# A causal mask added by VectorE in the maximum pass of an attention kernel, and a narrower last diagonal tile

## The chip, the cores and the metric

The kernel runs on one core of a Trainium2 chip. The metric is the device time of one execution in microseconds (us). Three runs of the kernel before gave 2625.49, 2625.82 and 2627.09 us; the median is 2625.82.

The engines are named as the profile names them: PE is TensorE (PEld its weight loads), DVE is VectorE, ACT is ScalarE, POOL is GpSimd, and SP is the queue that issues nearly all DMAs. Each engine works through its own queue in order and waits on semaphores for the others.

## The reference, cut to what matters

One decoder layer on 2048 tokens of 1024 channels: attention and a state-space model side by side, an output projection, a gated feed-forward network. Only the attention is touched here. It has 8 heads of 64 channels, is causal, and adds a forgetting bias to the scores:

```
cum = jnp.cumsum(log_f, axis=1).transpose(0, 2, 1)
...
    s = jnp.einsum('bqhd,bkhd->bhqk', q_i, k,
                   preferred_element_type=jnp.float32) * scale
    s = s + cum_i[..., :, None] - cum[:, :, None, :]
    mask = kpos[None, :] <= qpos[:, None]
    s = jnp.where(mask, s, NEG_INF)
    p = jax.nn.softmax(s, axis=-1)
    return jnp.einsum('bhqk,bkhd->bqhd', p.astype(v.dtype), v)
```

All data are float32, and the result has to be accurate to float32. So the kernel splits an operand into a high part of type float32r and the remainder, also as float32r, and multiplies the parts (high by high, high by low, low by high).

## The kernel before, in words

**Tiling.** The 2048 tokens are four blocks of 512 (`TB`). Attention is worked off by pairs of query block b and head h: 4 x 8 = 32 pairs, called heads below. For a pair the key blocks 0 to b are needed, the diagonal one (key block b) first.

**Two passes.** The softmax needs the row maximum before the exponentials.

- The *maximum pass*, `att_max` (L932 to L975), has scores with queries on the partitions. For each key block `ch` and each of four query tiles `s` of 128 rows, one matmul (L954) gives up to 512 key columns in a PSUM tile, from the high parts alone, with two more contraction rows that bring the forgetting bias. On the diagonal block only the first max(256, (s+1) x 128) columns are computed, and a second matmul (L958) adds the mask: it multiplies a bf16 identity, `identb`, by the bf16 tile `mask_q`, which holds 0 or -1e30, and accumulates into the columns s x 128 and on (256 columns wide for s = 0, otherwise 128). VectorE then takes the maximum of each row (L959) into a column of `mx`. `finish_max` (L961) reduces `mx` to the negated maximum, transposes it and stores it by DMA in row 66 of `qa`, so that the main pass subtracts it inside a matmul.
- The *main pass*, `att_main` (L979 to L1070), has scores with keys on the partitions. For each key block and each of four key tiles `i`, two matmuls (L997, L998) build scores minus maximum; on the diagonal block a third adds the mask from `mask_t`. There the columns start at `c0 = min(i * P, 256)`: 512, 384, 256 and 256 columns for i = 0 to 3. Tile i = 3 has only 128 valid columns; its mask (L1001) is 256 wide, and the first half of it is -1e30 throughout; the others use a mask of 128 columns (L1003). Then ScalarE takes the exponential into `pf` (L1007, two buffers) and makes its high part `ph` (L1008), VectorE makes the low part `pl` (L1009) and adds `pf` to the running row sums `acc` (L1014 for the first tile, L1017), and TensorE multiplies `ph` and `pl` by the values into `o_ps` (L1018, L1022).

**Score buffers.** Both passes take PSUM tiles from `am_ps` (L269): two buffers `sc_ps`, and from block 1 on also `qs_ps` and `vq_ps` in turn.

**What sets the order.** `attention` (L1072) writes out the order by hand: while a head is in its main pass, the steps of the next head's maximum pass are dealt out between its steps. Block 0's attention is emitted after the state-space model, which is issued at high priority, and stands beside it and the projections of blocks 2 and 3. The attention of blocks 1 to 3 (L1738) stands beside the output projection of block 0 and the first feed-forward matmuls (`up`, L1258), which fill TensorE between its steps. The whole program goes through a planner (`schedule_with_timeline_sim=True`, L1922): it puts the instructions of each engine in order by priority and by its own estimates of their times.

**Other lines named below.** L329: conditioning; L87: low part of a weight; L439 and L472: input projection, with L478 for the low part of queries and keys; L853, L859: state-space model; L555, L590: forget gates; L1147: GpSimd fills the constant rows of the tiles `qa`, `ka`, `kx`; L1048: reciprocals of the row sums; L1232, L1290 to L1292: output and down projections. `rsqrt_mean` (L172) is a chain of small VectorE operations.

Of the kernel before, what the change touches and what calls it, by code (L numbers as in the profile page):

```python
# [22 lines left out]
P = 128  # L23
# [11 lines left out]
NEG = -1e30  # L35
# [85 lines left out]
def hybrid_layer(ctx, tc, x, c_t, w_ada, b_col, gains, w_flat, bf_row, a_re, a_im, log_dt,  # L121
# [21 lines left out]
    identb = const.tile([P, P], BF16, name="identb")  # L143
# [5 lines left out]
    for g in range(2):  # L149
        G.memset(sel[g * 64 : (g + 1) * 64, g : g + 1], 1.0)  # L150

    mask_t = const.tile([P, 2 * P], BF16, name="mask_t")
    G.memset(mask_t, 0.0)
    G.affine_select(out=mask_t[:, P : 2 * P], in_=mask_t[:, P : 2 * P], pattern=[[1, P]],
                    compare_op=ALU.is_ge, fill=NEG, base=0, channel_multiplier=-1)
    G.memset(mask_t[:, 0:P], NEG)
    mask_q = const.tile([P, 2 * P], BF16, name="mask_q")
    G.memset(mask_q, 0.0)
    G.affine_select(out=mask_q[:, 0:P], in_=mask_q[:, 0:P], pattern=[[-1, P]],
                    compare_op=ALU.is_ge, fill=NEG, base=0, channel_multiplier=1)  # L160
    G.memset(mask_q[:, P : 2 * P], NEG)

    gain = const.tile([P, 32], F32, name="gain")
    Q.dma_start(gain, gains)
# [767 lines left out]
    def att_max(b, h):  # L932
# [16 lines left out]
        def part(ch, s):  # L949
            if s == 0:  # L950
                load(ch)
            n = max(256, (s + 1) * P) if ch == b else 512
            ps = max_ps()
            T.matmul(ps[:, 0:n], lhsT=qa[0:66, s * P : (s + 1) * P], rhs=ka[ch][0:66, 0:n], start=True,  # L954
                     stop=(ch != b))
            if ch == b:
                m0, mn = s * P, (2 * P if s == 0 else P)
                T.matmul(ps[:, m0 : m0 + mn], lhsT=identb, rhs=mask_q[:, 0:mn], start=False, stop=True)  # L958
            V.reduce_max(out=mx[:, s, ch : ch + 1], in_=ps[:, 0:n], axis=AX.X)  # L959

        def finish_max():  # L961
            mneg = small.tile([P, 4], F32, name="mneg", tag="mneg")
# [16 lines left out]
    def att_main(b, h, qa, qb, ka):  # L979
# [4 lines left out]
        def part(ch, i):  # L984
# [12 lines left out]
            T.matmul(ps[:, cs], lhsT=kbt[:, ks], rhs=qb[:, cs], start=True, stop=False)  # L997
            T.matmul(ps[:, cs], lhsT=ka[ch][:, ks], rhs=qa[:, cs], start=False, stop=(ch != b))  # L998
            if ch == b:
                if i == 3:  # L1000
                    T.matmul(ps[:, 256:512], lhsT=identb, rhs=mask_t, start=False, stop=True)  # L1001
                else:
                    T.matmul(ps[:, c0 : c0 + P], lhsT=identb, rhs=mask_t[:, P : 2 * P], start=False, stop=True)  # L1003
# [3 lines left out]
            A.activation(pf[:, cs], ps[:, cs], AF.Exp)  # L1007
            A.copy(ph[:, cs], pf[:, cs])  # L1008
            V.tensor_tensor(out=pl[:, cs], in0=pf[:, cs], in1=ph[:, cs].bitcast(F32), op=ALU.subtract)  # L1009
            first = state["first"]  # L1010
# [916 lines left out]
```

## Time and profile before

| what | value |
|---|---|
| median of 3 runs | 2625.82 us |
| profiled execution, its span | 2625.8 us |
| instructions | 35861 |
| mean granted TensorE clock | 0.980 |
| matmuls | 12235 |
| mask matmuls of the maximum pass (L958) | 128 |
| mask matmuls of the main pass (L1001, L1003) | 32 and 96 |
| maximum reductions (L959) | 320 |
| exponentials (L1007) | 320 |

The profiled execution took as long as the runs, so its durations can be set against the median as they are.

How the views are read. The page's first part gives for each engine the busy time, its share of the span and the instructions; the 40 slices show the busy share in tenths along the span. A row by line or by form gives the line, the engine, the operation, output <- inputs with their shapes, the count, the busy time and the mean of one in ns, and then the idle time just before these instructions with what ended it. A row of the waits gives who waited for whom, the total in us, how often and the longest. A row of one source line gives the minimum, median and maximum of one in ns and the first and last start. A row of the timeline begins with the start and the duration in us; for a matmul the duration runs from its start until its result is out, so that matmuls overlap in it, and what one costs the next is the distance between their starts.

### The profile page before, as it was taken

The page shows a single profiled execution, that of the slowest core. Times are in us where ns is not written, and L with a number is a line of the kernel's source. Part 1 is how long each engine was busy: PE and PEld are TensorE (multiplying, and loading weights), DVE is VectorE, ACT ScalarE, POOL GpSimd, SP SyncE. Part 2 cuts the span into 40 slices and gives each one's busy share as a digit, 9 for nine tenths or more (in the row PEclk, how much of TensorE's full clock was granted, in tenths as well). Part 3 has the DMA queues.
Part 4 walks back from the last instruction along what each step waited for, and adds up shares of the span by engine and source line. Part 5 has one row for each costly group of instructions (what it writes and reads, how often), then busy time and mean ns, then how long its engine had stood idle before and what let it go on. Part 6 is the DMA issues. An engine that isn't in the chain of part 4 may idle for free.

```text
span 2625.8 us, 35861 instructions
## 1 busy us (share of the span) xinstructions
PE 2539.7 (97%) x12235; PEld 2056.0 (78%) x12235; DVE 2043.4 (78%) x3824; ACT 1257.6 (48%) x2120; POOL 145.9 (6%) x130
## 2 busy tenths in 40 slices
PE   6999999998999999999999999999989999999997
PEld 3888877887788787888778888888767888887776
DVE  7989688966887878787877777776589888876777
ACT  3423255644454545455545555556554555543213
POOL 0001000000000000000000000000002333320000
PEclk8899999998999999999999999999999999999998
DMA  9476986667556655556557555556733443447573
GB/s 318 150 250 217 299 263 199 198 190 236 173 190 215 199 184 184 191 178 207 176 196 224 184 171 192 170 182 225 245 103 128 168 153 136 153 144 289 190 277 119
DMA packets 269319, 516.37 MB, mean 197 GB/s; under 512 B 27952, under 2 KB 114864, under 8 KB 269136
## 3 DMA queue, kind: packets, MB, share of 16 engines
q1 hardware_dynamic: 267312, 508.84, 58.4%
q0 software_dynamic: 1280, 4.20, 0.4%
q8 instruction: 97, 1.59, 0.3%
q10 hardware_dynamic: 544, 1.05, 0.1%
q14 instruction: 86, 0.70, 0.1%
HBM read 374.32 MB, written 139.59 MB: 196 GB/s over the span
## 4 chain that ended last, share of the span: by engine, by line
PE 80%; DMA 7%; DVE 7%; issue 2%; ACT 2%; SPq 1%; POOL 0%; DVEq 0%; POOLq 0%; ACTq 0%
PE ff_ps L1258 19%; PE up_x L1382 7%; PE ff_ps L1232 7%; PE up_z L1382 5%; PE up_y L1382 4%; PE ff_ps L1290 3%; PE ff_ps L1292 3%; PE ff_ps L1291 3%; PE o_ps L1018 2%; PE o_ps L1022 2%; DMA wada<-in_w_ada 2%; PE proj_ps L439 2%; PE acc_x L1612 2%; PE vq_ps L472 2%; PE qs_ps L472 2%
## 5 line engine op out<-in xcount | busy, mean ns | idle before, releaser
L86 ACT CAST w_hi<-w_raw 128x1024 fp32r<-128x1024 f32 (+4 forms) x187 | 173.1, 927 | 270.5 <-DMA w_raw<-in_w_flat 71.6
L1258 PE MATMUL ff_ps<-h_lo,w_hi 128*128 128x512 f32 x704 | 279.8, 397 | 0.8 <-DVE h_lo L391 0.8
L1258 PE MATMUL ff_ps<-h_hi,w_lo 128*128 128x512 f32 x704 | 280.0, 398 | 0.0
L1258 PE MATMUL ff_ps<-h_hi,w_hi 128*128 128x512 f32 x704 | 279.8, 399 | 0.0
L87 DVE TENSOR_TENSOR w_lo<-w_raw,w_hi 128x1024 fp32r<-128x1024 f32 (+4 forms) x187 | 199.8, 1069 | 64.4 <-ACT w_hi L86 52.5
L1009 DVE TENSOR_TENSOR pl<-pf,ph 128x512 fp32r<-128x512 f32 (+1 forms) x320 | 194.9, 618 | 19.8 <-ACT ph L1008 17.1
L1008 ACT CAST ph<-pf 128x512 fp32r<-128x512 f32 (+1 forms) x320 | 177.9, 569 | 62.4 <-PE o_ps L1018 56.4
L1017 DVE TENSOR_TENSOR acc<-acc,pf 128x512 f32<-128x512 f32 (+2 forms) x264 | 159.2, 605 | 26.0 <-ACT pf L1007 23.5
L1007 ACT ACTIVATE pf<-sc_ps 128x512 f32<-128x512 f32 (+2 forms) x184 | 98.3, 539 | 123.3 <-PE sc_ps L998 74.7
L1258 PEld LDWEIGHTS ff_ps<-h_lo,w_hi 128*128 128x128 f32 x704 | 133.6, 190 | 29.5 <-DVE h_lo L391 1.1
L1258 PEld LDWEIGHTS ff_ps<-h_hi,w_lo 128*128 128x128 f32 x704 | 133.5, 190 | 28.8
L1258 PEld LDWEIGHTS ff_ps<-h_hi,w_hi 128*128 128x128 f32 x704 | 133.4, 190 | 28.6 <-issue 0.2
L116 ACT CAST w_hi<-w_raw 128x1024 fp32r<-128x1024 f32 (+2 forms) x100 | 96.4, 964 | 103.7 <-PE ff_ps L1232 41.9
L1291 PE MATMUL ff_ps<-act_lo,w_hi 128*128 128x512 f32 x352 | 139.6, 397 | 0.0
L1290 PE MATMUL ff_ps<-act_hi,w_hi 128*128 128x512 f32 x352 | 139.4, 398 | 0.2 <-ACT rt L378 0.2
L1292 PE MATMUL ff_ps<-act_hi,w_lo 128*128 128x512 f32 x352 | 139.4, 397 | 0.0
L959 DVE TENSOR_REDUCE mx<-sc_ps 128x1 f32<-128x512 f32 (+2 forms) x164 | 97.6, 599 | 52.4 <-PE sc_ps L958 25.9
L1018 PE MATMUL o_ps<-ph,vv 128*128 128x512 f32 (+1 forms) x320 | 121.2, 380 | 2.2 <-ACT ph L1008 2.2
L1022 PE MATMUL o_ps<-pl,vv 128*128 128x512 f32 (+2 forms) x312 | 116.2, 375 | 0.9 <-DVE pl L1009 0.9
L1382 PE MATMUL up_x<-hh,w_hi 128*128 128x512 f32 x352 | 112.7, 400 | 3.4 <-ACT hh L387 1.8
L1364 POOL TENSOR_TENSOR s<-v_raw 128x512 f32<-128x512 f32 x18 | 27.7, 1538 | 1518.9 <-DVE w_lo L87 1518.9
L86 ACT CAST w_hi<-s 128x1024 fp32r<-128x1024 f32 (+2 forms) x66 | 62.1, 944 | 81.8 <-DVE s L1583 31.7
(678 smaller groups left out, 6961.1 us busy)
## 6 DMA issues: line engine op xcount, KB each, us to landing
w_raw<-in_w_flat SPq DMA_DIRECT2D x193, 512.0 KB
w_lo<-wlo SPq DMA_DIRECT2D x68, 512.0 KB
wlo<-w_lo SPq DMA_DIRECT2D x52, 512.0 KB
kb<-kb SPq DMA_DIRECT2D x80, 256.0 KB
vv<-v SPq DMA_DIRECT2D x80, 256.0 KB
w_raw<-in_w_flat SPq DMA_DIRECT2D x40, 384.0 KB
w_raw<-in_w_flat SPq DMA_DIRECT2D x40, 320.0 KB
wada<-in_w_ada SPq DMA_DIRECT2D x48, 256.0 KB
```

Source lines behind the costliest of these rows:

```text
L86: nc.scalar.copy(hi[:, :n], raw[:, :n])
L87: nc.vector.tensor_tensor(out=lo[:, :n], in0=raw[:, :n], in1=hi[:, :n].bitcast(F32), op=ALU.subtract)
L1008: A.copy(ph[:, cs], pf[:, cs])
L1009: V.tensor_tensor(out=pl[:, cs], in0=pf[:, cs], in1=ph[:, cs].bitcast(F32), op=ALU.subtract)
L1018: T.matmul(o_ps[:, cs], lhsT=vt[:, i, :], rhs=ph[:, cs], start=first, stop=False)
L1022: T.matmul(o_ps[:, cs], lhsT=vt[:, i, :], rhs=pl[:, cs], start=False, stop=(b > 0 and ch == b - 1 and i == 3))
L1232: mark[0] = T.matmul(ps, lhsT=lt, rhs=rt, start=(i == 0), stop=(i == 23))
L1258: T.matmul(ps, lhsT=lt, rhs=rt, start=(n == 0), stop=(n == 23))
L1290: T.matmul(ps, lhsT=a, rhs=ah[:, ts], start=(c == 0), stop=False)
L1291: T.matmul(ps, lhsT=a, rhs=al[:, ts], start=False, stop=False)
L1292: mark[0] = T.matmul(ps, lhsT=bb, rhs=ah[:, ts], start=False, stop=(c == n - 1))
L1382: mark[0] = T.matmul(ps, lhsT=lt, rhs=rt, start=(first and n == 0), stop=(n == 11), skip_group_check=not first)
```

## The change

In the maximum pass the mask matmul (L958) is gone. For the diagonal block VectorE adds `mask_q` to the scores in PSUM, writes the sum back in place and takes the maximum, in one instruction (`tensor_tensor_reduce`) on (s+1) x 128 columns. `mask_q` is now 512 columns wide, with the triangle in its last 128; its slice `(3 - s) * P` and on lines up with the query tile.

In the main pass the mask matmul of tile i = 3 is 128 wide, like the others. The exponential reads only the 128 valid columns of that tile, and GpSimd fills the other 128 of `pf` with zeros. `mask_t` is 128 columns wide. In `rsqrt_mean` two tiles have two buffers each, where they had four.

```
-    mask_t = const.tile([P, 2 * P], BF16, name="mask_t")
+    mask_t = const.tile([P, P], BF16, name="mask_t")
...
-    mask_q = const.tile([P, 2 * P], BF16, name="mask_q")
+    mask_q = const.tile([P, 4 * P], BF16, name="mask_q")
     G.memset(mask_q, 0.0)
-    G.affine_select(out=mask_q[:, 0:P], in_=mask_q[:, 0:P], pattern=[[-1, P]],
+    G.affine_select(out=mask_q[:, 3 * P :], in_=mask_q[:, 3 * P :], pattern=[[-1, P]],
                     compare_op=ALU.is_ge, fill=NEG, base=0, channel_multiplier=1)
-    G.memset(mask_q[:, P : 2 * P], NEG)
...
-        i = small.tile([P, 8], I32, name="rs_i")[:, :n]
+        i = small.tile([P, 8], I32, name="rs_i", bufs=2)[:, :n]
...
-            t = small.tile([P, 8], F32, name="rs_t")[:, :n]
+            t = small.tile([P, 8], F32, name="rs_t", bufs=2)[:, :n]
...
-            T.matmul(ps[:, 0:n], lhsT=qa[0:66, s * P : (s + 1) * P], rhs=ka[ch][0:66, 0:n], start=True,
-                     stop=(ch != b))
+            T.matmul(ps[:, 0:n], lhsT=qa[0:66, s * P : (s + 1) * P], rhs=ka[ch][0:66, 0:n], start=True, stop=True)
+            to = mx[:, s, ch : ch + 1]
             if ch == b:
-                m0, mn = s * P, (2 * P if s == 0 else P)
-                T.matmul(ps[:, m0 : m0 + mn], lhsT=identb, rhs=mask_q[:, 0:mn], start=False, stop=True)
-            V.reduce_max(out=mx[:, s, ch : ch + 1], in_=ps[:, 0:n], axis=AX.X)
+                sc = ps[:, 0 : (s + 1) * P]
+                V.tensor_tensor_reduce(out=sc, in0=sc, in1=mask_q[:, (3 - s) * P :], scale=1.0, scalar=3.0 * NEG,
+                                       op0=ALU.add, op1=ALU.max, accum_out=to)
+            else:
+                V.reduce_max(out=to, in_=ps[:, 0:n], axis=AX.X)
...
             if ch == b:
-                if i == 3:
-                    T.matmul(ps[:, 256:512], lhsT=identb, rhs=mask_t, start=False, stop=True)
-                else:
-                    T.matmul(ps[:, c0 : c0 + P], lhsT=identb, rhs=mask_t[:, P : 2 * P], start=False, stop=True)
+                T.matmul(ps[:, i * P : (i + 1) * P], lhsT=identb, rhs=mask_t, start=False, stop=True)
...
-            A.activation(pf[:, cs], ps[:, cs], AF.Exp)
+            e0 = i * P if ch == b else 0
+            if e0 > c0:
+                G.memset(pf[:, c0:e0], 0.0)
+            A.activation(pf[:, e0:], ps[:, e0:], AF.Exp)
```

More of the change, by code (lines that the diff above doesn't have):

```diff
@@ L150, in hybrid_layer @@
         G.memset(sel[g * 64 : (g + 1) * 64, g : g + 1], 1.0)
-    mask_t = const.tile([P, 2 * P], BF16, name="mask_t")
+    mask_t = const.tile([P, P], BF16, name="mask_t")
     G.memset(mask_t, 0.0)
-    G.affine_select(out=mask_t[:, P : 2 * P], in_=mask_t[:, P : 2 * P], pattern=[[1, P]],
-                    compare_op=ALU.is_ge, fill=NEG, base=0, channel_multiplier=-1)
-    G.memset(mask_t[:, 0:P], NEG)
-    mask_q = const.tile([P, 2 * P], BF16, name="mask_q")
+    G.affine_select(out=mask_t, in_=mask_t, pattern=[[1, P]], compare_op=ALU.is_ge, fill=NEG, base=0,
+                    channel_multiplier=-1)
+    mask_q = const.tile([P, 4 * P], BF16, name="mask_q")
     G.memset(mask_q, 0.0)
-    G.affine_select(out=mask_q[:, 0:P], in_=mask_q[:, 0:P], pattern=[[-1, P]],
+    G.affine_select(out=mask_q[:, 3 * P :], in_=mask_q[:, 3 * P :], pattern=[[-1, P]],
                     compare_op=ALU.is_ge, fill=NEG, base=0, channel_multiplier=1)
-    G.memset(mask_q[:, P : 2 * P], NEG)
     gain = const.tile([P, 32], F32, name="gain")
```

## The prediction

> **What bounds the kernel now.** I read the page from the top: busy time by engine, the 40 slices, the chain that ended last.
>
> ```profile
> PE 2539.7 (97%) x12235; PEld 2056.0 (78%) x12235; DVE 2043.4 (78%) x3824; ACT 1257.6 (48%) x2120; POOL 145.9 (6%) x130
> PE   6999999998999999999999999999989999999997
> PE 80%; DMA 7%; DVE 7%; issue 2%; ACT 2%; SPq 1%; POOL 0%; DVEq 0%; POOLq 0%; ACTq 0%
> ```
>
> TensorE is busy nearly everywhere and is four fifths of the chain. The edit touches attention alone, so the next view is the windows, cut at the attention of block 0 (313 to 650 us) and of blocks 1 to 3 (650 to 1830 us).
>
> ```profile
> core 0: us, PE busy (x) PEld busy (x) DVE busy (x) ACT busy (x) POOL busy (x), PEclk, DMA share, GB/s
> 0.00:313.00 313.00, 279.44 (x1669) 233.67 (x1670) 262.91 (x731) 101.73 (x202) 20.13 (x47) 0.93 0.75 244
> 313.00:650.00 337.00, 322.35 (x1866) 267.39 (x1865) 258.26 (x514) 166.26 (x338) 2.07 (x4) 0.96 0.74 224
> 650.00:1830.00 1180.00, 1172.79 (x5370) 941.48 (x5369) 903.95 (x1653) 645.61 (x1077) 0.00 (x0) 1.00 0.57 189
> 1830.00:2626.00 796.00, 765.08 (x3335) 613.49 (x3333) 618.31 (x926) 343.97 (x504) 123.75 (x79) 0.99 0.50 177
> ```
>
> From 650 to 1830 us TensorE rests 1180 - 1173 = 7 us, less than 1%, at a full clock; VectorE is busy 904 of 1180 (77%), ScalarE 646 (55%), GpSimd never. In block 0's attention TensorE has 322 of 337 (96%). The busy time of pipelined matmuls is modelled, so I also look at the waits of TensorE, first from 650 to 1830 us, then from 313 to 650 us (the longest lines).
>
> ```profile
> PE o_ps L1018 <- ACT ph L1008: 2.2, 2, 1.7
> PE o_ps L1022 <- DVE pl L1009: 0.9, 1, 0.9
> PE sc_ps L954 <- DVE mx L959: 0.8, 1, 0.8
> ```
> ```profile
> PE vq_ps L439 <- DVE qk_lo L478: 3.8, 2, 3.2
> PE qs_ps L954 <- DVE mx L959: 3.4, 1, 3.4
> ```
>
> TensorE waits for the maximum in two places, 4.2 us in all. So a matmul slot taken out of attention shortens the kernel, unless VectorE's or GpSimd's new work makes a new wait.
>
> **Part 1, the mask matmuls of the maximum pass.** L958 goes: one for each head and query tile, 32 x 4 = 128. This is its line of the code, by output buffer:
>
> ```profile
> L958 PE MATMUL sc_ps<-mask_q,identb x81: 219/232/287, 315.7 to 1717.3; 128*128 128x128 bf16 x61, 128*128 128x256 bf16 x20
> L958 PE MATMUL vq_ps<-mask_q,identb x25: 229/232/331, 629.3 to 1708.7; 128*128 128x128 bf16 x17, 128*128 128x256 bf16 x8
> L958 PE MATMUL qs_ps<-mask_q,identb x22: 230/231/285, 623.5 to 1656.6; 128*128 128x128 bf16 x18, 128*128 128x256 bf16 x4
> ```
>
> 81 + 25 + 22 = 128. Their 0.23 us is the time from start to result; matmuls overlap. What one costs TensorE is read from the distance between starts, in the timeline of TensorE at 1001 us:
>
> ```profile
> 1000.62 0.34 PE L998 MATMUL qs_ps<-qa,ka 67*128 67x384 f32 x1
> 1000.80 0.23 PE L1003 MATMUL qs_ps<-mask_t,identb 128*128 128x128 bf16 x1
> 1000.84 0.47 PE L1258 MATMUL ff_ps<-h_hi,w_hi 128*128 128x512 f32 x1
> 1001.16 0.28 PE L954 MATMUL sc_ps<-ka,qa 66*128 66x256 f32 x1
> 1001.28 0.28 PE L958 MATMUL sc_ps<-mask_q,identb 128*128 128x256 bf16 x1
> 1001.32 0.36 PE L954 MATMUL sc_ps<-ka,qa 66*128 66x256 f32 x1
> 1001.51 0.39 PE L1018 MATMUL o_ps<-ph,vv 128*128 128x512 f32 x1
> 1001.75 0.23 PE L958 MATMUL sc_ps<-mask_q,identb 128*128 128x128 bf16 x1
> 1001.78 0.48 PE L1258 MATMUL ff_ps<-h_lo,w_hi 128*128 128x512 f32 x1
> 1002.10 0.39 PE L1258 MATMUL ff_ps<-h_hi,w_lo 128*128 128x512 f32 x1
> 1002.33 0.40 PE L1258 MATMUL ff_ps<-h_hi,w_hi 128*128 128x512 f32 x1
> ```
>
> An undisturbed matmul of 512 columns holds its place 0.23 us (1002.10 to 1002.33), one of 256 columns 0.12 (1001.16 to 1001.28). A mask matmul is followed after 0.03 to 0.04 us, but the matmul behind it then holds its place longer: 1001.78 to 1002.10 is 0.32 instead of 0.23, and the one of 256 columns, 1001.32 to 1001.51, 0.19 instead of 0.12. Mask and follower together cost 1002.10 - 1001.75 - 0.23 = 0.12 us more, 1001.51 - 1001.28 - 0.12 = 0.11, and 1001.16 - 1000.80 - 0.23 = 0.13. I take 0.12 us, whatever the mask's width: the weights of the mask and of its follower have to go in behind a matmul too short to cover them. After a score matmul of only 256 columns without a mask (1001.16) no such loss shows, so nothing takes its place.
>
> The Trainium skill has another price for this: "TensorE: Matmul & The Clock Gate", section "Back-to-back issue gap", gives about 81 ns for a matmul of 128 columns with its weight load, by which the sum below would be 128 x 0.081 = 10.4 us (an estimate from that page). The distances between starts here are 0.11 to 0.13 us, so the trace decides against it.
>
> The sum: 32 of the 128 lie in block 0's attention, where TensorE sets the pace for 96% of the time: 32 x 0.12 x 0.96 = 3.7 us. The other 96 lie where it does for 99%: 96 x 0.12 x 0.99 = 11.4 us. Together 15.1 us off the path.
>
> **Part 2, the maximum on VectorE.** The mask is now added while the maximum is taken, on 128, 256, 384 and 512 columns instead of 256, 256, 384 and 512, and the sum is written back into PSUM. No row shows this instruction. Its neighbours:
>
> ```profile
> L959 DVE TENSOR_REDUCE mx<-sc_ps 128x1 f32<-128x512 f32 x103 | 70.5, 686 | 39.0 <-PE sc_ps L954 25.9 <-PE sc_ps L958 12.8
> L959 DVE TENSOR_REDUCE mx<-sc_ps 128x1 f32<-128x256 f32 x45 | 18.4, 417 | 4.6 <-PE sc_ps L958 4.4
> L853 DVE TENSOR_TENSOR m<-ss_ps,tab 128x512 f32<-128x512 f32 x16 | 11.0, 687 | 9.4 <-PE ss_ps L848 9.2
> L590 DVE TENSOR_TENSOR fg<-fg 128x128 fp32r<-128x128 f32 x1 | 0.3, 284 | 0.0
> L1048 DVE RECIPROCAL rd<-sc_ps 128x8 f32<-128x8 f32 x12 | 2.4, 203 | 1.3 <-PE sc_ps L1046 1.2
> ```
>
> A two-input operation with a PSUM input takes as long as the reduction (687 against 686 ns), so the pass over the columns costs the same, and the first tile saves 417 - 284 = 0.13 us: 32 x 0.13 = 4.3 us less VectorE time as the lower bound. The upper bound is a separate small step to write the maximum out, at the 0.20 us of L1048: 128 x 0.20 - 4.3 = 21 us more. I take the middle of these, about +9 us, since nothing is nearer to either end. Even +21 us raises VectorE in attention from (258 + 904) / 1517 = 77% to 78%, so the cover that hides it is TensorE's own work. What is queued behind it on VectorE are the `pl` and `acc` of the main pass, whose readers are TensorE and ScalarE; and the score buffer is released later by the same 0.1 us. TensorE's wait for that is 4.2 us now; scaled by 0.1 of 0.69 us it grows by 0.6, and the maximum starts earlier because no mask matmul comes between. I charge 0.3 us.
>
> On that extra step the Trainium skill speaks against the change: "VectorE: DVE Perf Modes", section "Two Vector instructions with no wait between them", says that an operation that also writes out its accumulator is two instructions. No row of this trace shows one; it argues for the upper half of the bounds, which the time does not feel as long as TensorE leads.
>
> **Part 3, the last diagonal key tile.** The mask there shrinks from 256 to 128 columns (32 matmuls, one a head). As seen above, a mask of 256 columns costs TensorE no more than one of 128, so nothing. The exponential reads 128 columns, not 256, and GpSimd fills the other 128 with zeros.
>
> ```profile
> L1007 ACT ACTIVATE pf<-sc_ps 128x512 f32<-128x512 f32 x123 | 73.2, 598 | 92.9 <-PE sc_ps L998 74.7 <-PE sc_ps L1003 7.5 <-DVE pl L1009 7.0
> L1007 ACT ACTIVATE pf<-sc_ps 128x256 f32<-128x256 f32 x41 | 15.7, 384 | 19.6 <-PE sc_ps L1001 12.2 <-DVE pl L1009 3.4 <-DVE acc L1014 2.1
> L555 POOL MEMSET fg<- 128x128 f32 x1 | 0.2, 199 | 13.2 <-DVE ada_acc L321 13.2
> ```
>
> The slope is (598 - 384) / 256 = 0.84 ns a column, so 128 columns take about 384 - 107 = 277 ns: 32 x 0.11 = 3.4 us less on ScalarE, which is not the bound: nothing. The fill takes 0.20 us, beside an exponential of 0.28, and both wait for the same release of `pf`: nothing, as long as GpSimd, idle here, has nothing ahead in its queue. If that cover is gone, it costs what rival 3 says. The masks themselves are built in the first microseconds; `rs_i` and `rs_t`, cut to two buffers, are a chain on one engine: nothing.
>
> **Sum.** The profiled execution lasted 2625.8 us, as does the median of the runs, so no correction between them. 2625.8 - 15.1 + 0.3 = 2611.0 us.
>
> **Rivals.** 1. *VectorE gives half back.* At the upper bound of 0.20 us a maximum, the score buffers come free later in the bursts where one head's four diagonal tiles follow each other. If 0.06 us of each 0.20 reaches TensorE: 128 x 0.06 = 7.7 us, so 2618 to 2619 us. For it: TensorE has waited for `mx` before. Against: only twice.
> 2. *Another order.* The kernel's order is planned anew from estimated times. TensorE rests 34 + 15 + 7 + 31 = 86 us over the four windows; an order that moves a tenth of that changes the time by 8 us either way: 2603 or 2619. If it loses all 15 us it ends at 2625: the change does nothing. That the slots were not TensorE's limit, its busy time being modelled, would give the same.
> 3. *Slower: the fill holds the exponent's path.* The next `ph` (L1008), and so `o_ps` (L1018) in TensorE's in-order queue, now wait for GpSimd, which waits until VectorE has let go of `pf`. ScalarE already waits for such a release, `pl`, for 7.0 us on these buffers. And in block 0's attention GpSimd's queue holds one fill that waited 236 us for VectorE's `gg`:
>
> ```profile
> 545.75 0.52 POOL L1147 MEMSET kx<- 3x512 f32 x1 [236.04 <-DVE gg L859]
> ```
>
> A `pf` fill ordered behind it waits with it. If each of 32 fills comes 1 us late, TensorE stands 32 us and the time is 2611 + 32 = 2643; it turns slower than before from 15 / 32 = 0.47 us a head. Against: the exponential waits for the same readers of `pf` anyway, and `gg` stands in VectorE's own queue with the attention's steps, so neither can run far ahead of the other.
>
> **How the numbers follow.** The forecast (2607 to 2616) gets 0.58; rival 1 0.12; a better order 0.09; a worse one 0.08; no gain 0.05; rival 3, or another wait as large, 0.08. The range 2602 to 2622 holds all but the last two and the tails. A change under 0.2% (5 us) can't be told from none here; faster by more than that means below 2620.6: 0.58 + 0.12 + 0.09 and half of the worse order, 0.83. Within 0.2%: the other half and no gain, 0.09. Slower: 0.08.
>
> **What would show it.** In the new profile: no L958 matmul; TensorE still over 99% busy from 650 us to the end of attention, which comes about 15 us earlier; the matmul behind a score matmul of the maximum pass back at 0.23 us; the new VectorE row near 285, 418, 551 and 686 ns, with or without a second short row; ScalarE's row of 128 columns near 277 ns; 32 GpSimd fills of 0.2 us that no engine waits for. I am wrong if TensorE's waits on `mx`, `ph` or GpSimd grow by several us, or if a window outside attention changes by as much.

## The result and the profile after

The changed kernel takes 2601.27 us (median of 4 runs, 2598.54 to 2602.08), the kernel before on the same chip 2625.65 (4 runs, 2624.64 to 2627.09). The ratio is 0.9912, with a 95% interval of 0.9898 to 0.9925. It is faster by 24.4 us where 14.8 were forecast; the time lies just below the range. The profiled execution spans 2600.4 us at a mean granted clock of 0.98.

From the page of the changed kernel, busy time by engine, TensorE's slices and the chain:

```profile
PE 2506.6 (96%) x12107; PEld 2046.8 (79%) x12107; DVE 2046.1 (79%) x3952; ACT 1253.3 (48%) x2120; POOL 152.2 (6%) x160
PE   5999899998999999999999999999989999999997
PE 81%; DVE 8%; DMA 6%; ACT 2%; issue 2%; SPq 1%; POOL 0%; POOLq 0%; DVEq 0%; ACTq 0%
```

128 matmuls are gone and VectorE has 128 instructions more, but only 2.7 us more of busy time; TensorE still sets the end. Now the windows, cut as before, with a fifth one inside the up projection (1990 to 2330 us), a stretch that the diff does not touch:

```profile
0.00:313.00 313.00, 275.20 (x1673) 230.47 (x1674) 262.48 (x731) 101.69 (x202) 19.93 (x45) 0.95 0.75 244
313.00:650.00 337.00, 320.50 (x1864) 269.60 (x1863) 263.26 (x561) 168.49 (x343) 3.71 (x12) 0.96 0.74 228
650.00:1830.00 1180.00, 1171.25 (x5337) 949.49 (x5336) 906.76 (x1766) 648.88 (x1087) 4.94 (x24) 0.99 0.59 194
1830.00:2626.00 796.00, 739.65 (x3240) 597.27 (x3238) 613.62 (x897) 334.19 (x489) 123.60 (x79) 0.98 0.48 168
1990.00:2330.00 340.00, 340.00 (x1481) 277.83 (x1481) 289.86 (x339) 171.57 (x234) 114.13 (x70) 1.00 0.40 145
```

The same stretch of the kernel before:

```profile
1990.00:2330.00 340.00, 340.00 (x1464) 275.35 (x1463) 288.33 (x339) 171.47 (x233) 112.78 (x68) 1.00 0.40 146
```

Here lies the surprise. In both kernels this window holds nothing on TensorE but matmuls of 512 columns of one line (L1382), TensorE never rests, and the granted clock is 1.00. Yet in 340 us the changed kernel does 1481 of them and the kernel before 1464: 340 / 1481 = 0.2296 us a matmul against 340 / 1464 = 0.2322. A matmul that nobody touched has become 2.7 ns faster.

Inside attention the predicted signs are there. TensorE's timeline of the changed kernel at 1004 us (start, duration):

```profile
1003.38 0.39 PE L1258 MATMUL ff_ps<-h_hi,w_lo 128*128 128x512 f32 x1
1003.61 0.34 PE L952 MATMUL vq_ps<-ka,qa 66*128 66x384 f32 x1
1003.79 0.40 PE L1258 MATMUL ff_ps<-h_hi,w_hi 128*128 128x512 f32 x1
1004.02 0.28 PE L997 MATMUL qs_ps<-qb,kb 128*128 128x256 f32 x1
...
1004.86 0.23 PE L1000 MATMUL qs_ps<-mask_t,identb 128*128 128x128 bf16 x1
1004.90 0.48 PE L1258 MATMUL ff_ps<-h_lo,w_hi 128*128 128x512 f32 x1
1005.22 0.40 PE L1258 MATMUL ff_ps<-h_hi,w_lo 128*128 128x512 f32 x1
```

Behind the score matmul of the maximum pass (L952, 1003.61) the next one holds its place 4.02 - 3.79 = 0.23 us. Behind a mask of the main pass, which is still there, it is 5.22 - 4.90 = 0.32.

The new VectorE instruction, from the view of its line (minimum, median and maximum in ns) and from the groups:

```profile
L956 DVE DVE_READ_ACCUMULATOR2_ANT mx<- x128: 82/141/145, 320.4 to 1703.7; 128x1 f32 x128
```
```profile
L956 DVE DVE_READ_ACCUMULATOR2_ANT mx<- 128x1 f32 x128 | 17.8, 139 | 0.0
L956 DVE CUSTOM_DVE_ANT_0 sc_ps<-sc_ps,mask_q 128x512 f32<-128x512 f32 x20 | 14.0, 698 | 8.4 <-PE sc_ps L952 8.4
L1007 ACT ACTIVATE pf<-sc_ps 128x128 f32<-128x128 f32 x18 | 5.0, 276 | 10.0 <-PE sc_ps L1000 8.8 <-DVE pl L1009 1.2
```

The second, short instruction exists, 128 of them at 139 ns, as the page of the Trainium skill cited in the prediction says ("VectorE: DVE Perf Modes", "Two Vector instructions with no wait between them"); the trace adds its price. The main instruction takes 291, 442, 564 and 697 ns for 128, 256, 384 and 512 columns, in the mean over all score buffers (forecast 285, 418, 551 and 686). ScalarE's exponential of 128 columns takes 276 ns (forecast 277). Whom GpSimd's fills hold up, and what TensorE waits for between 650 and 1830 us (the longest):

```profile
L1006 POOL MEMSET pf<- x32: 204/205/210, 343.0 to 1757.4; 128x128 f32 x32
...
who waited for it (us, times):
busy tenths in 40 slices 0000000000000000000000000000000000000000
```
```profile
PE o_ps L1022 <- DVE pl L1009: 2.3, 4, 0.8
PE vq_ps L952 <- DMA qa<-qb: 1.3, 1, 1.3
PE o_ps L1018 <- ACT ph L1008: 1.2, 3, 0.5
PE ff_ps L1258 <- DMA w_lo<-wlo: 1.0, 1, 1.0
PE sc_ps L952 <- ACT pf L1007: 0.7, 2, 0.4
PE ff_ps L356 <- DVE rs_y L183: 0.6, 1, 0.6
PE vq_ps L952 <- DVE mx L956: 0.5, 1, 0.5
```

From 313 to 650 us the two longest are these:

```profile
PE vq_ps L437 <- DVE qk_lo L476: 4.9, 2, 4.7
PE ff_ps L356 <- DVE rs_y L183: 3.4, 1, 3.4
```

The list of those who wait for a fill is empty, and between 650 and 1830 us no wait of TensorE has grown by several us. In block 0's attention the wait of 3.4 us for the maximum is gone, and one of 3.4 us for the small VectorE chain of `rsqrt_mean` (`rs_y`) has come. That the chain's tiles now have two buffers is not the cause: so they have in e1 and e5 below, which keep the old order of instructions, and among the eight longest waits of these stretches there is none for `rs_y`, but one of 4.0 and 3.9 us for the maximum.

### The profile page after: what moved, and what is told of

Its sections match the earlier page's. It is cut to its first block, busy times and chain, and to the rows that moved or that the text cites. A ratio compares the mean times of both kernels' runs of the same rounds, so it can differ in the third digit from the quotient of the medians.

```text
span 2600.4 us, 35785 instructions
## 1 busy us (share of the span) xinstructions
PE 2506.6 (96%) x12107; PEld 2046.8 (79%) x12107; DVE 2046.1 (79%) x3952; ACT 1253.3 (48%) x2120; POOL 152.2 (6%) x160
## 4 chain that ended last, share of the span: by engine, by line
PE 81%; DVE 8%; DMA 6%; ACT 2%; issue 2%; SPq 1%; POOL 0%; POOLq 0%; DVEq 0%; ACTq 0%
PE ff_ps L1258 18%; PE ff_ps L1232 7%; PE up_x L1382 7%; PE up_z L1382 4%; PE up_y L1382 4%; PE ff_ps L1290 3%; PE ff_ps L1292 3%; PE ff_ps L1291 3%; PE o_ps L1018 2%; PE o_ps L1022 2%; PE acc_x L1612 2%; PE vq_ps L470 2%; PE qs_ps L470 2%; DMA wada<-in_w_ada 2%; PE proj_ps L437 2%
## 5 line engine op out<-in xcount | busy, mean ns | idle before, releaser
L1007 ACT ACTIVATE pf<-sc_ps 128x512 f32<-128x512 f32 (+3 forms) x184 | 96.3, 528 | 128.3 <-PE sc_ps L998 76.1
L1382 PE MATMUL up_x<-hh,w_hi 128*128 128x512 f32 x352 | 112.0, 398 | 3.4 <-ACT hh L385 1.9
L1382 PE MATMUL up_z<-hh,w_hi 128*128 128x512 f32 x308 | 97.6, 398 | 2.9 <-ACT w_hi L86 2.9
L437 PE MATMUL proj_ps<-wu_hi,h_hi 128*128 128x264 f32 (+1 forms) x256 | 76.2, 304 | 13.4 <-ACT h_hi L388 11.7
```

The costliest lines, as they stand in the source:

```text
L1382: mark[0] = T.matmul(ps, lhsT=lt, rhs=rt, start=(first and n == 0), stop=(n == 11), skip_group_check=not first)
```

## The experiments

In this section "the old program" is the kernel before and "the new program" the kernel after. Each kernel was timed beside the kernel before on the same chip: e1 to e4 on one chip, e5 to e8 on a second, e9 to e11 on a third and e12 on a fourth, on which the kernel before took 2622.72, 2623.46, 2623.91 and 2622.91 us. So a difference between kernels of two of these groups is uncertain by 1 us from the chips alone. TensorE carries out its matmuls in the order of the kernel that each is derived from, one by one, in e1 to e5 and e9 to e12; e6 to e8 were planned anew.

The first question was why the up projection is faster. The diff changes the sizes of `mask_t` and `mask_q` (256 bytes a partition more in all) and gives two small tiles fewer buffers (128 less), and everything allocated behind them moves. In the built programs the tiles `h_hi`, `h_lo`, `act` and a part of `hh`, which stream through TensorE as moving operands, go from 59072 (the lowest `h_hi`) to 59200, all by 128 bytes: the operands of 6516 of the 8584 float32r matmuls of 512 columns; the weights move by 256. Taken modulo 256, the moving operands go from remainder 192 to 64 and the weights stay at 64. Nearly all of the attention's operands and the rest of `hh` are allocated from the other end and stay where they are, most of them at 160.

**e1 and e2: program and addresses apart.** e1 is the old program with the new addresses:

```
-    mask_q = const.tile([P, 2 * P], BF16, name="mask_q")
+    mask_q = const.tile([P, 3 * P], BF16, name="mask_q")
...
-        i = small.tile([P, 8], I32, name="rs_i")[:, :n]
+        i = small.tile([P, 8], I32, name="rs_i", bufs=2)[:, :n]
...
-            t = small.tile([P, 8], F32, name="rs_t")[:, :n]
+            t = small.tile([P, 8], F32, name="rs_t", bufs=2)[:, :n]
```

> The program of before, instruction for instruction in the same order, with the SBUF addresses of after: the mask tile of the maximum pass is 768 bytes wide instead of 512 (its last third unused), and the two small tiles of the square root have two buffers. So the weight tiles lie 256 bytes higher and the tiles h, act, hh and yt of the left side 128 bytes higher, as in after; the attention's tiles on the right side don't move. Theory 'layout' (part of the gain is that matmuls with 512 moving columns hold TensorE 229 ns in after where they hold it 232.6 in before, since their operands lie elsewhere): 5561 such matmuls by 3.5 ns less is 19 us, the 1500 of the attention lose 1 ns or 1.5 us, so about 2608 us. Rival 'order': the gain beyond the mask slots comes from the new order of instructions; then this is no faster than before, 2625 us. Rival 'slots alone': also 2625 us.

Measured: 2610.27 us (2604.16 to 2615.94, 6 runs) against 2622.72 for the kernel before, ratio 0.9955 (0.9938 to 0.9972). e2 is the new program with the old addresses:

```
-    mask_t = const.tile([P, P], BF16, name="mask_t")
+    mask_t = small.tile([P, P], BF16, name="mask_t", bufs=1)
...
-            mneg = small.tile([P, 4], F32, name="mneg", tag="mneg")
+            mneg = small.tile([P, 4], F32, name="mneg", tag="mneg", bufs=2)
...
-            rd = small.tile([P, 8], F32, name="rd", tag="rd")
+            rd = small.tile([P, 8], F32, name="rd", tag="rd", bufs=2)
```

> The program of after, in the same order, with the matmul operands at the SBUF addresses of before: the 256 bytes of the narrow mask lie in the pool of small tiles, and two more small tiles (the negated maximum and the reciprocals) have two buffers instead of four. Theory 'layout': the 512-column matmuls hold TensorE 232.6 ns again, so about 2601 + 18 = 2619 us, 6 to 8 us faster than before only. Forecast of the prediction, slots alone: 2611 us. Rival 'order': 2601 us, as after.

Measured: 2614.71 us (2608.87 to 2621.45, 12 runs), ratio 0.9969 (0.9958 to 0.9979). The window of the up projection, first e1, then e2:

```profile
1990.00:2330.00 340.00, 340.00 (x1481) 277.70 (x1480) 291.83 (x340) 172.49 (x236) 118.88 (x72) 1.00 0.40 145
```
```profile
1990.00:2330.00 340.00, 340.00 (x1465) 275.15 (x1464) 289.85 (x337) 169.85 (x233) 116.93 (x72) 1.00 0.40 143
```

The count goes with the addresses (1481 and 1465), not with the program. So there are two causes of like size: the addresses alone are worth 12.5 us, the program alone 8.0.

**e3 and e5: which addresses.** e3 is the old program with more buffers for another small tile, so that only what lies behind the weights moves (`h_hi` to 59200, weights where they were). e5 is the old program with only the two small tiles cut (`h_hi` at 58944, again remainder 64, with the weights again unmoved).

```
-            r = small.tile([P, 8], F32, name="rs_y")[:, :n]
+            r = small.tile([P, 8], F32, name="rs_y", bufs=8)[:, :n]
```

> The program of before, in the same order, with only the left-side tiles h, act, hh and yt 128 bytes higher, as in after, and the weight tiles where they were: the small tile of the square root's result has eight buffers instead of four. If the moving operand's own address counts (its remainder by 256 goes from 192 to 64), this is as fast as the first of these kernels, about 2608 us. If what counts is where moving operand and weights lie to each other (their distance modulo 2048 is 128 bytes in before, 0 in after, 256 here), it is not: 2625 us, or slower. If addresses don't count: 2625 us.

Measured: 2608.91 us (2605.41 to 2616.99, 6 runs), ratio 0.9951 (0.9936 to 0.9966).

```
-        i = small.tile([P, 8], I32, name="rs_i")[:, :n]
+        i = small.tile([P, 8], I32, name="rs_i", bufs=2)[:, :n]
...
-            t = small.tile([P, 8], F32, name="rs_t")[:, :n]
+            t = small.tile([P, 8], F32, name="rs_t", bufs=2)[:, :n]
```

> The program of before in the same order, with one line of the change alone: the two small tiles of the square root have two buffers instead of four. That puts the left-side tiles 128 bytes lower than in before (they were 128 higher in the changed kernel); the weights stay. If the moving operand's address counts by its remainder modulo 256 (192 in before, 64 here and in after), the 512-column matmuls hold TensorE 229 ns and the time is 12 to 14 us below before, near 2609 us. If it is the absolute place, or the distance to something that stays, it is not: 2623 us. If addresses are no cause at all: 2623 us.

Measured: 2610.17 us (2606.28 to 2613.28, 5 runs) against 2623.46, ratio 0.9952 (0.994 to 0.9965). Whether the weights move by 256 bytes (e1) or stay (e3, e5) does not matter, nor does the direction of the move. (Modulo 256 the weights of these matmuls are at 64 in all three; other remainders of theirs were not tried.) The matmul itself is shorter: in the up projection, the kernel before and then e3, as groups (count, busy us, mean ns of one),

```profile
L1382 PE MATMUL up_y<-h_hi,w_lo 128*128 128x512 f32 x68 | 26.9, 396 | 0.0
```
```profile
L1382 PE MATMUL up_y<-h_hi,w_lo 128*128 128x512 f32 x72 | 28.0, 389 | 0.0
```

396 against 389 ns from start to result, for the same instruction on the same data.

**e4: the changed kernel again**, unedited, beside e1 to e3.

> The changed kernel itself, on the same chip as the three others, so that they are compared on one chip. All theories: 2601 us. Rival 'chip' (the difference in matmul spacing is one between chips): then it need not be 2601, and before on the same chip moves as well.

Measured: 2598.02 us (2595.1 to 2600.89, 4 runs), ratio 0.9906 (0.9892 to 0.9921), against 0.9912 on the chip of the first result, so the gain does not come from the chip. With new addresses on both sides, e4 against e1, the program is worth 2610.27 - 2598.02 = 12.3 us; with old addresses, e2 against the kernel before, 8.0.

**e6 and e7: the two parts of the program alone**, both with `h_hi` at remainder 64, so that the measure is the old program there, 2610.2 us (e5, same chip). e6 has the new maximum pass and the old main pass:

```
             if ch == b:
-                m0, mn = s * P, (2 * P if s == 0 else P)
-                T.matmul(ps[:, m0 : m0 + mn], lhsT=identb, rhs=mask_q[:, 0:mn], start=False, stop=True)
-            V.reduce_max(out=mx[:, s, ch : ch + 1], in_=ps[:, 0:n], axis=AX.X)
+                sc = ps[:, 0 : (s + 1) * P]
+                V.tensor_tensor_reduce(out=sc, in0=sc, in1=mask_q[:, (3 - s) * P :], scale=1.0, scalar=3.0 * NEG,
+                                       op0=ALU.add, op1=ALU.max, accum_out=to)
+            else:
+                V.reduce_max(out=to, in_=ps[:, 0:n], axis=AX.X)
```

> The changed maximum pass with the main pass of before (mask of 256 columns in the last diagonal tile, exponential on 256 columns, no fill by GpSimd); the left-side tiles lie at remainder 64 as in after, with three more small tiles cut to two buffers to make room. Prediction: the maximum part carries the whole gain of the slots, the main part nothing, so this is as fast as after, 2598 us, within 2 us and the change of the order. Rival: the main part gives a part (shorter ScalarE path at the end of each diagonal): 2601 to 2604 us.

Measured: 2604.41 us (2601.07 to 2608.36, 5 runs), ratio 0.993 (0.9917 to 0.9942). e7 has the new main pass and the old maximum pass:

```
-                if i == 3:
-                    T.matmul(ps[:, 256:512], lhsT=identb, rhs=mask_t, start=False, stop=True)
-                else:
-                    T.matmul(ps[:, c0 : c0 + P], lhsT=identb, rhs=mask_t[:, P : 2 * P], start=False, stop=True)
+                T.matmul(ps[:, i * P : (i + 1) * P], lhsT=identb, rhs=mask_t, start=False, stop=True)
...
-            A.activation(pf[:, cs], ps[:, cs], AF.Exp)
+            e0 = i * P if ch == b else 0
+            if e0 > c0:
+                G.memset(pf[:, c0:e0], 0.0)
+            A.activation(pf[:, e0:], ps[:, e0:], AF.Exp)
```

> The changed main pass with the maximum pass of before (mask matmuls); the left-side tiles lie at remainder 64 as in after. Prediction: the main part is worth nothing on TensorE, so this is as fast as the old program at the new addresses, 2610 us. Rival: the fill by GpSimd holds the exponent's path: over 2613 us. Rival: the shorter exponential helps: 2605 us.

Measured: 2607.54 us (2603.56 to 2610.02, 5 runs), ratio 0.994 (0.9928 to 0.9953). The main part is worth 2.6 us, with runs that overlap e5's, so it can't be told from nothing; the fills hold nobody up. The maximum part is worth 5.8 us (2601.07 to 2608.36 against e5's 2606.28 to 2613.28, so this size is uncertain too) and not the 12 that e6's expectation gave it. The two make 8.4, where the whole program gave 12.3 on the other chip. Whether the new order of e6 and e7 or the scatter of the runs makes that difference is not shown.

**e8: the old program with every mask matmul of the maximum pass issued twice** (the mask is added twice, and a masked score only gets lower).

```
+                T.matmul(ps[:, m0 : m0 + mn], lhsT=identb, rhs=mask_q[:, 0:mn], start=False, stop=False)
                 T.matmul(ps[:, m0 : m0 + mn], lhsT=identb, rhs=mask_q[:, 0:mn], start=False, stop=True)
```

> Before, at its own addresses, with every mask matmul of the maximum pass issued twice (128 more; masked scores become -2e30). If a mask slot costs 0.12 us of TensorE's time, 15 us more than before, 2638 us; a second mask directly behind the first may cost only its weight load, 0.07 us, so 9 us more, 2632 us, as the lower bound. If the mask slots were hidden: 2623 us.

Measured: 2647.69 us (2645.18 to 2651.37, 4 runs), ratio 1.01 (1.0085 to 1.0116): 24 us slower. TensorE's timeline of e8 shows why this is no price list:

```profile
1003.25 0.36 PE L954 MATMUL sc_ps<-ka,qa 66*128 66x256 f32 x1
1003.45 0.28 PE L958 MATMUL sc_ps<-mask_q,identb 128*128 128x256 bf16 x1
1003.57 0.27 PE L959 MATMUL sc_ps<-mask_q,identb 128*128 128x256 bf16 x1
1003.60 0.48 PE L1019 MATMUL o_ps<-ph,vv 128*128 128x512 f32 x1
1003.91 0.28 PE L954 MATMUL sc_ps<-ka,qa 66*128 66x256 f32 x1
```

A mask in front of another holds its place for its columns (0.12 us for 256), and the loss falls on the long matmul behind the last one (3.91 - 3.60 = 0.31). From start of the first mask to the end of the follower's place, two masks of 128 columns ahead of a matmul of 512 take 411 ns where one takes 355 (medians of 45 cases in e8 and 53 in the kernel before), those of 256 columns 466 against 356 (16 and 15 cases): 96 x 0.056 + 32 x 0.110 = 9 us by these places, as in the lower bound. (That bound named a weight load of 0.07 us; no row shows one of that length, the loads of these masks take 0.10 us.) The other 15 us are not at the masks. In the profiled executions the stretch from the first score matmul to the first matmul of the up projection holds the same matmuls in both kernels but for the 128 added masks, and takes 1636.1 us instead of 1614.1. By the count explained below (under "The mask slots"), the masks and the matmuls behind them take 7.8 us more of it, and the distances behind all other matmuls 14.1. The plan is new: attention ends at 1812.0 us instead of 1828.4, with feed-forward matmuls left for later. That the new plan is the cause of the 14 us is likely, but not shown. Mask matmuls do cost time in this kernel; the size can't be read from e8.

**e9 and e10: other remainders.** The new program, with the moving operands of projections and feed-forward at remainder 0 (e9) and 128 (e10).

```
-            mneg = small.tile([P, 4], F32, name="mneg", tag="mneg")
+            mneg = small.tile([P, 4], F32, name="mneg", tag="mneg", bufs=2)
```

> The changed kernel in its own order, with the left-side tiles 64 bytes lower (remainder 0 modulo 256 instead of 64; one more small tile has two buffers). Measures the third point of the spacing of 512-column matmuls against the remainder of the moving operand's address: 64 gave 229.0 ns, 192 gave 232.6. If the rule is alignment to 128 or 256 bytes, 0 is at least as fast as 64: 227 to 229 ns and 2598 us or less. If 64 is a special place: 232 ns and 2613 us.

Measured: 2614.47 us (2612.43 to 2622.3, 5 runs) against 2623.91, ratio 0.9962 (0.9948 to 0.9975).

```
-        mx = small.tile([P, 4, NB], F32, name="mx", tag="mx")
+        mx = small.tile([P, 4, NB], F32, name="mx", tag="mx", bufs=2)
...
-            mneg = small.tile([P, 4], F32, name="mneg", tag="mneg")
+            mneg = small.tile([P, 4], F32, name="mneg", tag="mneg", bufs=2)
```

> The same with the left-side tiles 192 bytes lower than in the changed kernel (remainder 128 modulo 256; two more small tiles have two buffers). If the two halves of 256 bytes differ (64 fast, 192 slow), 128 goes with 192: 232 to 233 ns and 2613 us. If alignment to 128 bytes counts: as fast as remainder 0.

Measured: 2605.12 us (2601.73 to 2608.75, 5 runs), ratio 0.9928 (0.9915 to 0.994). The window of the up projection, e9 and then e10:

```profile
1990.00:2330.00 340.00, 340.00 (x1461) 273.33 (x1460) 287.40 (x336) 170.16 (x231) 115.26 (x70) 1.00 0.40 146
```
```profile
1990.00:2330.00 340.00, 340.00 (x1471) 276.15 (x1470) 289.57 (x338) 171.55 (x234) 115.75 (x71) 1.00 0.40 144
```

The largest power of two is not the best place: remainder 0 is as slow as 192, as the second of e9's two cases had it. 128 lies between, where neither case of e10's expectation had put it. Over the whole trace I joined each matmul with its operand's address in the built program and took the distance to the next start, for pairs of 512 columns in float32r that follow within 250 ns, by the remainder of the first one's operand:

| remainder of the moving operand | mean distance, pairs | kernel | median of the new program, us |
|---|---|---|---|
| 64 | 229.2 ns, 6085 | e4 | 2598.0 |
| 128 | 230.6 ns, 6063 | e10 | 2605.1 |
| 192 | 232.6 ns, 6113 | e2 | 2614.7 |
| 0 | 233.0 ns, 6082 | e9 | 2614.5 |

From 192 to 64 that is 3.4 ns x 6100 = 21 us on TensorE. About 2 us of it are lost again at the operands that stay at 160 (1480 pairs, 232.9 ns in e2, 234.1 in e4), which leaves 19, of which 16.7 are found in the time (12.5 in the old program). From 128 to 64 it is 1.4 ns x 6070 = 8 us, and 7.1 are found, 5.9 of them beyond the difference of the two chips.

**e11 and e12: the attention's operands at remainder 64 as well.** An unused tile of 96 bytes ahead of them moves all of these from 160 to 64. e11 is the new program, e12 the old one with the same addresses throughout.

```
-    vq = opened(vq_ctx, "vq", bufs=2, side="right")
+    pad = ctx.enter_context(tc.tile_pool(name="pad", bufs=1, side="right")); pad.tile([P, 24], F32, name="pad"); vq = opened(vq_ctx, "vq", bufs=2, side="right")
...
-        mx = small.tile([P, 4, NB], F32, name="mx", tag="mx")
+        mx = small.tile([P, 4, NB], F32, name="mx", tag="mx", bufs=2)
...
-            mneg = small.tile([P, 4], F32, name="mneg", tag="mneg")
+            mneg = small.tile([P, 4], F32, name="mneg", tag="mneg", bufs=2)
...
-            rd = small.tile([P, 8], F32, name="rd", tag="rd")
+            rd = small.tile([P, 8], F32, name="rd", tag="rd", bufs=2)
```

> The changed kernel with the right-side tiles (attention's qa, ka, qb, kb, vv, ph, pl and the late operands of the up projection) 96 bytes lower: their remainder goes from 160 to 64, where the left side's tiles lie as well. The order of the instructions is planned anew, since some reused spaces now border on others. If remainder 64 is fast for them too, their 1500 matmuls go from 234 to 229 ns, 7 us less: 2591 us, faster than before and after. If 160 was no handicap: 2598 us, give or take the new order.

Measured: 2588.74 us (2585.28 to 2589.57, 4 runs) against 2623.91, ratio 0.9863 (0.985 to 0.9877): 35 us under the kernel before and the fastest of all. The order of the matmuls came out as in the new program, other than expected. e12 has the same four edits and those of e1.

> The kernel before, with its instructions in their old order and both masks still added by TensorE, but with the addresses of e11 throughout: the operands of the projections and of the feed-forward, and those of the attention, all at remainder 64. It measures what the change of the program is worth a third time, as the distance between this run and e11, and it asks whether the gain by addresses belongs to the matmuls or to the new program. Theory (addresses and program are two separate terms): the attention's operands are worth the same 12.5 us to the old program as to the new one, so about 2610.3 - 12.5 = 2598 us by e1; the program part is then 2598 - 2588.7 = 9 us, between the 8 us of e2 against before and the 12 us of e4 against e1, and the ratio to the kernel before is 0.990. Rival 1 (the program part is the 15 us of the prediction and the two smaller figures come from layouts): 2588.7 + 15 = 2604 us. Rival 2 (the attention's addresses help only where no mask matmul stands between the matmuls): close to e1, 2608 to 2611 us. In the trace the distance between the starts of 512-column matmuls in attention is 0.229 us by the theory, 0.234 us by rival 2.

Measured: 2602.03 us (2599.11 to 2604.36, 5 runs) against 2622.91, ratio 0.9913 (0.99 to 0.9927). Its window of the up projection, in which a part of `hh` lies on the attention's side:

```profile
1990.00:2330.00 340.00, 339.76 (x1491) 279.44 (x1490) 290.83 (x340) 171.51 (x234) 116.16 (x71) 1.00 0.40 146
```

1491 instead of 1481. The pairs whose operand stayed at 160 gained nothing when the others moved (232.9 and 234.1 ns, above); they even lost a little, so a matmul's distance depends to some degree on its neighbours' operands too. In e11 and e12 nearly all operands are at 64, and the mean over 7567 and 7503 pairs there is 228.9 ns. The clearest pair is inside the up projection, where the weights stay at 64: the part of `hh` on the attention's side goes from 234.0 ns in e4 (493 pairs, remainder 160) to 227.1 in e11 (492 pairs, 64), while the part that was at 64 before goes from 227.6 to 228.5. The distance goes with the operand that is moved, in the old program as in the new, so rival 2 of e12's expectation is out. It is not the distance between moving operand and weights: for the operands of projections and feed-forward it is 0 modulo 256 in e1, e3, e4 and e5, the fast ones, but also in 292 pairs of e4 that have both at 160, and these take 233.8 ns. Nor is it the remainder modulo 256 alone: in e11 and e12 some 280 pairs have their operand at 128, and their mean is 232.7 ns, not the 230.6 of e10.

The addresses alone are worth 2622.9 - 2602.0 = 21 us to the old program, nearly as much as the whole change gave. And the program is worth 2602.03 - 2588.74 = 13.3 us in this layout (14.3 when each of the two is set against the kernel before on its own chip). That lies between the 9 us of e12's theory and the 15 of its rival 1, the prediction's figure, and nearer to the second.

## Why the prediction was right and where it failed

**The step that failed: the side effects at "nothing".** Part 3 let the changed buffers pass: "`rs_i` and `rs_t`, cut to two buffers, are a chain on one engine: nothing", and the masks were only "built in the first microseconds". I looked at what these lines compute and not at where they put everything behind them. They move the moving operands of 6516 matmuls by 128 bytes, and that is worth 12 to 14 us in the old program (e1, e3, e5) and 16.7 in the new (e4 against e2). The prediction's own test caught it: it said that I am wrong if a window outside attention changes by as much, and the up projection did. The direction came out right with a term missing that happened to have the same sign. That the time ended only 0.7 us below the range is luck of the same kind: the missing term is as large as the forecast gain, and the forecast gain came out smaller.

**The mask slots (15.1 us): right in their price, not in what becomes of the freed time.** The places are as forecast: in the median a mask's own 0.04 us and 0.083 to 0.087 more for its follower before, 0.23 behind a score matmul after. But three pairs that differ in the program alone give 8.0 (e2 against the kernel before), 12.3 (e4 against e1) and 13.3 us (e11 against e12), a mean of 11.2, where 14.8 was forecast. The profiled executions show where the rest went. From the first score matmul to the first matmul of the up projection the two programs have the same matmuls but for the 128 masks (7652 and 7524 records). For every matmul I took the distance from its start to the next one's, and as its norm the median for its number of columns and type over both programs of the pair. What a distance has beyond the norm is called excess.

| us, old program to new | before, e2 | e1, e4 | e12, e11 |
|---|---|---|---|
| length of the stretch | 1614.1 to 1604.0 | 1605.8 to 1593.0 | 1598.4 to 1585.4 |
| masks' own places | 15.0 to 0 | 14.6 to 0 | 12.1 to 0 |
| excess of their followers | 11.9 to 0 | 12.1 to 0 | 12.2 to 0 |
| excess of all other matmuls | 81.8 to 98.6 | 78.4 to 92.3 | 95.5 to 106.9 |

So 24 to 27 us are freed, more than the sum of the medians, and 11 to 17 come back at other matmuls. The step that Part 1 had wrong is its factors of 0.96 and 0.99, by which nearly all of a freed slot is time won because TensorE is busy. A piece of what reappears is the wait for `rs_y` in block 0's attention, 2.9 to 3.9 us in the four profiles of the new program that I asked (the kernel after, e2, e4, e11); another has gone there, the wait for the maximum, 3.4 to 4.0 us in the old (before, e1, e5, e12). What sets the rest is open. The pair of e2 gives some 5 us less than the others and has the largest return, 16.8 us; why is open as well. Single runs of one kernel scatter by 6 to 7 us to either side (e2: 2608.87 to 2621.45), so a part of it may be no difference at all. The Trainium skill's 81 ns would have given 10.4 us, nearer to the mean of 11.2; the distances measured here, before and after, still do not bear out 81 ns.

For the reason of the price, weights that have to go in behind a matmul too short to cover them, the weight loads of the kernel before speak at the mask of 1001.75 us:

```profile
1001.74 0.10 PEld L958 LDWEIGHTS <-identb 128*128 128x128 bf16 x1
1001.75 0.20 PEld L1258 LDWEIGHTS ff_ps<-h_lo,w_hi 128*128 128x128 f32 x1
1001.87 0.19 PEld L1258 LDWEIGHTS ff_ps<-h_hi,w_lo 128*128 128x128 f32 x1
```

The follower's load takes 0.20 us and starts with the mask, so it ends at 1001.95, while the mask's place ends at 1001.78. The next load, 0.19 us, starts at 1001.87 under that long matmul and is over at 1002.06, before its own matmul starts at 1002.10. This fits the reason; no run here changes the load alone.

**VectorE.** From VectorE's timeline of the changed kernel:

```profile
1003.99 0.57 DVE L956 CUSTOM_DVE_ANT_0 vq_ps<-vq_ps,mask_q 128x384 f32<-128x384 f32 x1 [0.83 <-PE vq_ps L952]
1004.47 0.14 DVE L956 DVE_READ_ACCUMULATOR2_ANT mx<- 128x1 f32 x1
1005.06 0.70 DVE L956 CUSTOM_DVE_ANT_0 sc_ps<-sc_ps,mask_q 128x512 f32<-128x512 f32 x1 [0.45 <-PE sc_ps L952]
1005.67 0.14 DVE L956 DVE_READ_ACCUMULATOR2_ANT mx<- 128x1 f32 x1
1005.67 0.42 DVE L1017 TENSOR_TENSOR acc<-acc,pf 128x256 f32<-128x256 f32 x1
```

The accumulator read starts before the main instruction ends (1004.47 against 1004.56), and the next instruction can start together with the read (both at 1005.67). Summed by duration, the maxima take 212.8 us in e11 (131.4 plain, 81.5 masked) and 197.6 in e12, 15 us more and in the upper half of the bounds, as argued from the Trainium skill; but overlapped like this VectorE's busy time rose by only 2.7 us (page, 2043.4 to 2046.1). That TensorE hardly waits for it was right: from 650 to 1830 us the list shows 0.5 us for the new maximum (L956) and 2.3 for `pl`, so rival 1 is out as a mechanism, though the size of the program part came near to what it named in the pair of e2.

**The main pass.** Nothing was forecast, and 2.6 us that can't be told from nothing was measured (e7). Rival 3, the fill that holds the exponent's path, is out: nobody waits for it.

**Another order (rival 2)** was right in kind: with a new plan the attention and what follows exchange work (in e8 attention ends 16 us earlier with twice the masks), and neither e6 and e7 beside e4 nor e8 add up by the removed or added places alone, by some 4 us in the first and 15 in the second. It is not what made the changed kernel better than forecast, since e1 and e3 keep the old order and have the gain.

**What stays open.** Why a remainder of 64 is better than 128, and that than 192 and 0, no run shows: the modulus of 256 only sorts the four places tried for these operands, others (32, 96) were not tried, and the pairs at 128 in e11 and e12 (232.7 ns) do not fit the order that it gives.

## What to carry to other kernels

A change in the size or the number of buffers of an on-chip tile can move all that is allocated behind it, as here, and may so change the speed of matmuls that the change doesn't touch: time an edit against the old program at the new addresses before the gain is put down to the edit. A stretch of one kind of matmul at full clock, counted in equal windows before and after, shows such a shift at once. And where TensorE leads, removed slots are worth their distance between starts less the time that reappears at other matmuls: here 8 to 13 us of a forecast of 15.

## What the runs showed of the hardware

- The distance between starts of 512-column matmuls of float32r depends on where the moving operand lies: 229.2 ns at remainder 64 modulo 256 (e4), 230.6 at 128 (e10), 232.6 at 192 (e2) and 233.0 at 0 (e9), and it does so with the weights unmoved (e3, e5). The remainder is not the whole rule (232.7 ns for the pairs at 128 in e11). Moving 8262 of the 8584 operands to 64 took 21 us from the old program (e12) without a change in what it computes or in its order of matmuls.
- `tensor_tensor_reduce` with its maximum written out is two VectorE instructions: 697 ns for 512 columns from PSUM and back, and 139 ns for the accumulator, most of which lies beside the instructions around it.
- A second mask matmul directly behind a first adds only about the time of its columns, 56 ns for 128 and 110 for 256 (e8, in the median), where a lone one costs 0.12 us whatever its width: the loss sits between it and the float32r matmul behind, whose weight load takes 0.19 to 0.20 us against 0.10 for the mask's.
